# Weight sums by accumulating DMAs, and a reordered end of the MLP, in a two-layer encoder kernel

## The chip, the cores and the metric

One core of a Trainium2 chip runs the whole program in one launch. The metric is the device time of one execution in microseconds, the median of several. The engines are PE (TensorE matmul, with its weight loads shown as PEld), DVE (VectorE), ACT (ScalarE), POOL (GpSimd) and SP (SyncE, which here only issues DMAs).

## The reference

The kernel computes two layers of an encoder on 512 tokens of width 1024, in float32. Per layer:

```
u = RMSNorm(h);  project u with w_in; dilated attention A; retention B
h = h + RMSNorm((sigmoid(ga) * (A @ w_att_out) + sigmoid(gb) * (B @ w_ret_out)) @ w_out)
h = h + RMSNorm(relu(RMSNorm(h) @ w_up)^2 @ w_down)            # the MLP, D_FF = 4096
h = h + sigmoid(RMSNorm(h) @ w_ple_gate) * RMSNorm(p[i] @ w_ple_proj)
```

The change is in the third line alone: in how the weights of the down projection are added up, and in the last eighth of that projection.

## The kernel before

Every matmul is done in three float32r passes: weights and activations are split into a high part (an ACT copy, L273) and the rest (a subtraction on DVE or POOL, L297), and the list HL (L291) names the three products that are kept.

Weights come as 128x1024 blocks of 512 KB in the order of PLAN. `load` (L246) brings raw blocks in from SP into the tag "R" with four buffers; `prefetch` (L266) splits them into "wt" tiles, of which there are five; `chunk` (L285) is called where PE needs a weight and asks for splits up to three items ahead. A weight's split therefore waits until PE is done with the item five places before it.

The up projection makes 32 chunks of 128 features. The down projection of the first seven eighths (UNITS = 7) goes by a Strassen-Winograd scheme in place of plain products: for each unit of 512 features, with token halves and feature halves as a 2x2 of blocks, seven products P1 to P7 replace eight. Some of them need sums of weight blocks: P5 takes b11 + b12, P7 takes b12 + b22, and a chain adds b22 to P5's sum for P6, and b21 to that for P4. `total` (L255) makes these four sums on POOL, in the tag "X" with two buffers. P1, P3 and P2 take single blocks. Per unit the order is up, P1, P5, up, P7, P6, up, P3, P4, up, P2. The products are added up over the units in `prod` (tag "V", L856), and after the last unit seven "folds" (FOLD, L807, run at L905 to L907 on DVE) combine them: the results are P2 and P3 for token tiles 0 and 1, and P4 and P5 for tiles 2 and 3, one for each half of the 1024 columns.

The last eighth of the features is multiplied plainly (L930 to L932), in what the text calls the tail: `row_job` runs the left half of the columns for all four token tiles, weight by weight, then the right half tile by tile. `evac_dn` (L919) adds (left) or subtracts (right) the result into `prod`, takes the sum of squares on ACT, multiplies by the gain (POOL for the left half, DVE for the right), and after the right half calls `pre_norm` (L389) with the residual row h, reloaded from DRAM at L908 to L910 into the tag "A". `pre_norm` makes the normalised row `un`, and queues `rest` (L404): eight transposes of `un` on PE into the two "tp" banks, and the split into `uT` (L412 on ACT, L413 on DVE). `step` (L321), called after each six matmuls, runs the first queued `rest` once it is `age` steps old (AGE_DN = 6 in the tail, eight or seven in the gate stage); `settle` runs what a group of tiles still lacks. The stage behind the tail is the PLE gate ("pg", L953): its first group needs tiles 0 and 1.

PE's order is as written. The order on the other engines and on SP's queue is made by a scheduler that works with its own costs and with priorities: functions under `soon` go ahead by PRIO = 300 places. Each engine's queue is in order on the chip.

Of the kernel before, what the change touches and what calls it, by code (L numbers as in the profile page):

```python
# [12 lines left out]
ALU = mybir.AluOpType  # L13
# [4 lines left out]
P = 128  # L18
S = 512
D = 1024  # L20
NL = 2
NT = S // P
# [19 lines left out]
ALL, PAIRS, ONES = ((0, 1, 2, 3),), ((0, 1), (2, 3)), ((0,), (1,), (2,), (3,))  # L42
# [3 lines left out]
AGE_DN = 6  # L46
# [9 lines left out]
UNITS = 7  # L56


def _dn(e, hf, k):
    return 8 * (e // 2) + 4 * hf + 2 * (e % 2) + k  # L60
# [27 lines left out]
PLAN = [(i,) + x for i in range(NL) for x in PLAN_LAYER]  # L88
# [3 lines left out]
def _items():  # L92
    out = []
    for i in range(NL):
        for kind, c in PLAN_LAYER:
            e = 2 * (c // 8) + c % 4 // 2
            if kind == "up" and c >= 4 and c // 4 <= UNITS:
                e, at = c // 4 - 1, c % 4
                b11, b21, b12, b22 = (CHUNK[i, "dn", _dn(e, hf, k)] for hf in range(2) for k in range(2))
                out.append(((i, "up", c), (CHUNK[i, "up", c],)))  # L100
                out += [((i, p, e), src) for p, src in (
                    (("P1", (b11,)), ("P5", (b11, b12))),
                    (("P7", (b12, b22)), ("P6", ("chain", b22))),
                    (("P3", (b22,)), ("P4", ("chain", b21))),
                    (("P2", (b21,)),),
                )[at]]
            elif kind != "dn" or e >= UNITS:
                out.append(((i, kind, c), (CHUNK[i, kind, c],)))
    return out


ITEMS = _items()
ITEM = {key: m for m, (key, _) in enumerate(ITEMS)}
LAST = {x: m for m, (_, src) in enumerate(ITEMS) for x in src if x != "chain"}


def _qk_cols(base, tile_no, ret):
# [81 lines left out]
def block(ctx: ExitStack, tc: tile.TileContext, x, pT, w, dl, gains, cs, lc, rel, eye, out):  # L199
    nc = tc.nc  # L200
# [11 lines left out]
    def blk(tag, shape, dt=F32, name="blk"):  # L212
        return big.tile(shape, dt, name=name, tag=tag, bufs=NAMES[tag])
# [7 lines left out]
    def bank(tag):  # L221
        b = banks[tag].pop(0)
        banks[tag].append(b)
        return b
# [18 lines left out]
    raw, wt, chain = {}, {}, {}  # L243
    loaded = [0, 0]

    def load(to):  # L246
        while loaded[0] < min(to, len(PLAN)):
            n = loaded[0]
            if len(raw) >= (4 if n < 4 or PLAN[n][1] in ("up", "dn") else 2):
                return  # L250
            raw[n] = blk("A" if n < 4 else "R", [P, D], name="raw")
            nc.sync.dma_start(raw[n], w[n * P:(n + 1) * P, :])
            loaded[0] += 1

    def total(key, src):  # L255
        if src[0] == "chain":
            r, b = chain["sum"], raw[src[1]]
            nc.gpsimd.tensor_tensor(r, r, b, op=ALU.add)  # L258
            return r
        r = blk("X", [P, D], name="wsum")  # L260
        nc.gpsimd.tensor_tensor(r, raw[src[0]], raw[src[1]], op=ALU.add)  # L261
        if key[1] == "P5":
            chain["sum"] = r
        return r

    def prefetch(to_raw, to_split):  # L266
        while loaded[1] < min(to_split, len(ITEMS)):
            m = loaded[1]
            key, src = ITEMS[m]
            load(max([n for n in src if n != "chain"]) + 1)  # L270
            r = raw[src[0]] if len(src) == 1 else total(key, src)
            t = wp.tile([P, 2, 1024], F32R, name="wt", tag="wt", bufs=5)
            nc.scalar.activation(t[:, 0, :], r, AF.Copy)  # L273
            n = src[-1]
            pool = len(src) == 1 and (PLAN[n][1] in POOL_LOW and n % POOL_MOD or PLAN[n][1:] in POOL_MORE)
            for sl in HALVES if pool else (slice(0, D),):
                low(nc.gpsimd if pool else nc.vector, t[:, 1, sl], r[:, sl], t[:, 0, sl])
            wt[m] = t
            loaded[1] += 1
            for n in src:  # L280
                if LAST.get(n) == m:
                    raw.pop(n, None)
        load(to_raw)

    def chunk(*key):  # L285
        m = ITEM[key]
        n = max(x for _, src in ITEMS[max(0, m - 3):m + 4] for x in src if x != "chain")
        prefetch(n + 3, m + 4)
        return wt[m]
# [3 lines left out]
    def low(eng, dst, src, hi, scale=1.0):  # L293
        if scale != 1.0:
            nc.vector.scalar_tensor_tensor(dst, src, scale, hi.bitcast(F32), op0=ALU.mult, op1=ALU.subtract)
        else:
            eng.tensor_tensor(dst, src, hi.bitcast(F32), op=ALU.subtract)  # L297
# [18 lines left out]
    def row_mm(ps, ch, j, lhs, k, t, first, last):  # L316
        for n, (a, b) in enumerate(HL):
            nc.tensor.matmul(ps, lhsT=lhs(a, k, t), rhs=ch[:, b, j * S:(j + 1) * S],  # L318
                             start=first and n == 0, stop=last and n == 2)

    def step(age=None):  # L321
        clock[0] += 1
        age = AGE if age is None else age
        if pending and clock[0] - pending[0][0] >= age:
            soon(pending.pop(0)[1])()
        tick()

    def row_job(keys, lhs, evac, groups=ALL, age=None):
        n = len(keys)
        chs = {}  # L330
        for grp in groups:
            if lhs is u_lhs:
                settle(grp)
            pss = [bank(ROW_BANKS[n]) for n in range(len(grp))]
            for c in range(len(keys)):
                if grp is groups[0]:
                    chs[c] = chunk(*keys[c])
                for t, ps in zip(grp, pss):
                    for j in range(2):
                        row_mm(ps, chs[c], j, lhs, 2 * c + j, t, c == 0 and j == 0, c == n - 1 and j == 1)  # L340
                    if c == n - 1:
                        evac(t, ps)
                    step(age)
# [27 lines left out]
    def soon(f, offset=None):  # L371
        offset = PRIO if offset is None else offset

        def g(*a):
            if not offset:
                return f(*a)
            with tc.high_priority(offset=offset):
                return f(*a)
        return g
# [5 lines left out]
    def settle(ts):  # L385
        while any(t in unready for t in ts):
            soon(pending.pop(0)[1])()
# [247 lines left out]
    def one_layer(i, h):  # L635
# [14 lines left out]
        for c in range(2):  # L650
            b = blk("G", [P, 2, S], name="lct")
# [86 lines left out]
        h = [blk("V", [P, D], name="h") for _ in range(NT)]  # L738
# [3 lines left out]
        for c in range(8):  # L742
            th = ths[c] if c in ths else b_gate(c)
            ps = bank("acc")
            t_job((i, "ro", c), ps, rhs=retT)
            m = t2("m")
            nc.vector.scalar_tensor_tensor(m, th, 1.0, ps, op0=ALU.add, op1=ALU.mult)
            nc.gpsimd.tensor_tensor(fb[c // 2][:, c % 2, :], m, fb[c // 2][:, c % 2, :], op=ALU.add)
        for c in range(8):
            src = fb[c // 2][:, c % 2, :]  # L750
# [31 lines left out]
        for hf in range(2):  # L782
            hsl = slice(hf * S, (hf + 1) * S)
            ch = chunk(i, "pp", hf)
            for t in range(NT):
                ps = bank(PP_BANKS[4 * hf + t])
# [19 lines left out]
        prod = {x: blk("V", [P, 2, S], name=f"sum{x}") for x in PROD}  # L806
# [4 lines left out]
        def dn_bank():  # L811
            b = dn_banks.pop(0)
            dn_banks.append(b)
            return b
# [44 lines left out]
        for j in range(2):  # L859
            settle(PAIRS[j])  # L860
            for c in range(EARLY):
                if not j:
                    early.append(bank(EARLY_BANKS[c]))
                t = chunk(i, "up", c)
# [8 lines left out]
        half_f = []  # L873
# [24 lines left out]
        for e in range(UNITS):  # L898
            ops = operands(*half_f)
            half_f = []  # L900
            for n, xs in enumerate((("P1", "P5"), ("P7", "P6"), ("P3", "P4"), ("P2",))):
                up_job(4 * e + 4 + n)
                for name in xs:
                    product(e, name, ops[name])
                    if e == UNITS - 1:  # L905
                        for to, of in FOLD.get(name, ()):
                            nc.vector.tensor_tensor(prod[to], prod[to], prod[of], op=ALU.add)  # L907
        for t in range(NT):  # L908
            h[t] = blk("A", [P, D], name="hr")
            nc.sync.dma_start(h[t], hm[t])  # L910

        acc = [[prod[x][:, t % 2, :] for x in (("P2", "P3"), ("P4", "P5"))[t // 2]] for t in range(NT)]
# [6 lines left out]
        def evac_dn(hf):  # L919
            @soon  # L920
            def f(t, ps):
                a = acc[t][hf]
                nc.vector.tensor_tensor(a, ps, a, op=ALU.subtract if hf else ALU.add)
                ssq[t][hf] = sumsq(a, t2("junk"), None if hf else 1e-6)
                (nc.vector if hf else nc.gpsimd).tensor_tensor(a, a, g_mpost[:, HALVES[hf]], op=ALU.mult)
                if hf:
                    pre_norm(h[t], t, None, upd_mlp(t, rstd_of(*ssq[t])))
            return f

        for hf in range(2):  # L930
            row_job([(i, "dn", _dn(UNITS, hf, k)) for k in range(2)],
                    lambda a, k, t: half_f[k][:, a, t * P:(t + 1) * P], evac_dn(hf), ONES if hf else ALL, AGE_DN)  # L932

        if not last:
            g_next = gain_row(5 * (i + 1))
# [19 lines left out]
        if last:  # L955
            t, f = NT - 1, evac_pg(1)
            for j in range(CUTS):
                cut = slice(j * S // CUTS, (j + 1) * S // CUTS)
                n = cut.stop - cut.start
                ps = bank("acc")  # L960
# [9 lines left out]
    h = [blk("V", [P, D], name="h") for _ in range(NT)]  # L970
# [25 lines left out]
    for i in range(NL):  # L996
        h = one_layer(i, h)
# [29 lines left out]
```

## Time and profile before

| | |
|---|---|
| time before, median of 3 (lowest to highest) | 1811.55 us (1811.48 to 1811.81) |
| the profiled execution | 1810.16 us |
| its span, first to last instruction | 1808.4 us |
| mean granted TensorE clock | 0.994 |
| busy: PE, DVE, ACT, POOL | 1773.1, 1215.8, 822.1, 496.1 us |
| PE in 40 slices, in tenths | 8999999999999999998999999999999999999989 |
| DMA, mean over the span | 134 GB/s |

Times are from one profiled execution and count from the span's start. A busy PE is not PE at its peak, since matmuls overlap: the interval from one to the next says how fast it goes. The granted clock is 1.00 at 2.4 GHz and 0.50 at 1.2 GHz, and a value between them is a stretch with some of both.

### The profile page before, as it was taken

How to read it: one execution, taken by the hardware profiler on the slowest of the kernel's cores; microseconds unless marked ns; L12 is line 12 of the kernel's file. 1: busy time of each engine (PE TensorE's matmuls, PEld its weight loads, DVE VectorE, ACT ScalarE, POOL GpSimd, SP SyncE). 2: the span in 40 equal slices, each digit the busy share in tenths (PEclk: the TensorE clock that was granted, in tenths of full speed). 3: DMA queues.
4: the chain of work that ended last, by engine and by line, in shares of the span. 5: the costliest groups of instructions: out<-in, count | busy, mean ns of one | idle time of the engine just before them, and what ended most of it. 6: DMA issues, size and time to landing. Idle time of an engine off the chain costs nothing.

```text
span 1808.4 us, 22117 instructions
## 1 busy us (share of the span) xinstructions
PE 1773.1 (98%) x8185; PEld 1466.0 (81%) x8185; DVE 1215.8 (67%) x1839; ACT 822.1 (45%) x1291; POOL 496.1 (27%) x370
## 2 busy tenths in 40 slices
PE   8999999999999999998999999999999999999989
PEld 6888788888888888887888887888888888888867
DVE  6676768743557787788556767677444677777873
ACT  4355454422456454544343555443234574544442
POOL 2312144301165222222023222442012642222130
PEclk9999999999999999999999999999999999999989
DMA  5554464432343222334246545554232422333231
GB/s 214 200 182 157 156 209 148 144 140 93 111 146 117 94 94 97 113 122 158 94 140 212 166 149 171 180 164 169 98 112 97 137 94 99 111 107 104 94 140 47
DMA packets 79165, 243.10 MB, mean 134 GB/s; under 512 B 10961, under 2 KB 19537, under 8 KB 79058
## 3 DMA queue, kind: packets, MB, share of 16 engines
q1 hardware_dynamic: 79058, 241.70, 39.9%
q8 instruction: 64, 1.05, 0.2%
q14 instruction: 43, 0.35, 0.1%
HBM read 208.10 MB, written 33.55 MB: 134 GB/s over the span
## 4 chain that ended last, share of the span: by engine, by line
PE 87%; DVE 5%; POOL 3%; ACT 2%; issue 1%; DMA 1%; SPq 0%; ACTq 0%; POOLq 0%
PE acc L308 27%; PE s L308 17%; PE acc L318 17%; PE acc L845 10%; PE tp L845 5%; PE tp L608 2%; POOL wt L297 2%; PE tp L540 2%; PE tp L503 2%; PE acc L867 1%; ACT wt L273 1%; PE tp L409 1%; PE s L521 1%; DVE wt L297 1%; PE s L522 1%
## 5 line engine op out<-in xcount | busy, mean ns | idle before, releaser
L308 PE MATMUL acc<-uT,wt 128*128 128x512 f32 x1920 | 472.9, 393 | 0.0
L308 PEld LDWEIGHTS acc<-uT,wt 128*128 128x128 f32 x1920 | 356.5, 188 | 71.5
L273 ACT ACTIVATE wt<-raw 128x1024 fp32r<-128x1024 f32 x278 | 293.4, 1056 | 225.6 <-PE acc L308 114.5
L297 DVE TENSOR_TENSOR wt<-raw,wt 128x1024 fp32r<-128x1024 f32 x211 | 291.6, 1389 | 131.5 <-ACT wt L273 130.6
L318 PE MATMUL acc<-wt,uT 128*128 128x512 f32 x1320 | 324.2, 399 | 4.0 <-DVE uT L413 1.7
L308 PE MATMUL s<-uT,wt 128*128 128x512 f32 x1392 | 324.7, 389 | 0.0
L308 PEld LDWEIGHTS s<-uT,wt 128*128 128x128 f32 x1392 | 261.3, 188 | 54.0
L297 POOL TENSOR_TENSOR wt<-raw,wt 128x512 fp32r<-128x512 f32 x134 | 184.9, 1401 | 409.8 <-ACT wt L273 370.6
L318 PEld LDWEIGHTS acc<-wt,uT 128*128 128x128 f32 x1320 | 248.1, 191 | 55.8 <-DVE uT L413 2.9
L845 PE MATMUL acc<-wt,op 128*128 128x512 f32 x792 | 188.0, 389 | 0.0
L845 PEld LDWEIGHTS acc<-wt,op 128*128 128x128 f32 x792 | 148.7, 188 | 30.8
L261 POOL TENSOR_TENSOR wsum<-raw 128x1024 f32<-128x1024 f32 x28 | 74.7, 2667 | 210.1 <-DMA raw<-in_w_dram 210.1
L258 POOL TENSOR_TENSOR wsum<-wsum,raw 128x1024 f32<-128x1024 f32 x28 | 71.1, 2539 | 167.6 <-DVE wt L297 167.6
L856 DVE TENSOR_TENSOR sumP<-acc,sumP 128x512 f32<-128x512 f32 x112 | 75.5, 686 | 61.6 <-PE acc L845 61.1
L884 ACT ACTIVATE relu<-s 128x512 f32<-128x512 f32 x60 | 35.5, 592 | 175.7 <-PE s L308 175.7
L297 DVE TENSOR_TENSOR wt<-wsum,wt 128x1024 fp32r<-128x1024 f32 x56 | 83.9, 1498 | 15.4 <-ACT wt L273 15.4
L845 PE MATMUL tp<-wt,op 128*128 128x512 f32 x384 | 92.3, 389 | 0.0
L308 PE MATMUL acc<-retT,wt 128*128 128x512 f32 x384 | 89.3, 389 | 0.0
L845 PEld LDWEIGHTS tp<-wt,op 128*128 128x128 f32 x384 | 72.1, 188 | 14.9
L308 PEld LDWEIGHTS acc<-retT,wt 128*128 128x128 f32 x384 | 72.1, 188 | 14.9
L300 ACT ACTIVATE rt<-rz 128x512 fp32r<-128x512 f32 x64 | 40.3, 632 | 90.0 <-DVE rz L590 89.5
L526 ACT ACTIVATE z<-z,nm 128x512 f32<-128x512 f32 x64 | 46.2, 722 | 56.6 <-DVE nm L525 56.3
(166 smaller groups left out, 2232.3 us busy)
## 6 DMA issues: line engine op xcount, KB each, us to landing
raw<-in_w_dram SPq DMA_DIRECT2D x292, 512.0 KB, 3.3
kk<-stk SPq DMA_DIRECT2D x128, 128.0 KB, 4.1
stq<-rr SPq DMA_DIRECT2D x16, 512.0 KB, 3.4
qs<-stq SPq DMA_DIRECT2D x128, 64.0 KB, 2.8
stk<-rr SPq DMA_DIRECT2D x16, 512.0 KB, 3.0
stv<-vr SPq DMA_DIRECT2D x16, 512.0 KB, 4.8
vh<-stv SPq DMA_DIRECT2D x16, 512.0 KB, 4.3
gain<-in_gains_dram SPq DMA_DIRECT2D x9, 512.0 KB, 3.8
```

Of the source, the lines that this page charges most:

```text
L258: nc.gpsimd.tensor_tensor(r, r, b, op=ALU.add)
L261: nc.gpsimd.tensor_tensor(r, raw[src[0]], raw[src[1]], op=ALU.add)
L273: nc.scalar.activation(t[:, 0, :], r, AF.Copy)
L297: eng.tensor_tensor(dst, src, hi.bitcast(F32), op=ALU.subtract)
L300: nc.scalar.activation(dst[:, 0], src, AF.Copy, scale=scale)
L308: nc.tensor.matmul(ps, lhsT=t[:, a, (off + k) * P:(off + k + 1) * P], rhs=r, start=k == 0 and n == 0, stop=k == kts - 1 and n == 2)
L318: nc.tensor.matmul(ps, lhsT=lhs(a, k, t), rhs=ch[:, b, j * S:(j + 1) * S], start=first and n == 0, stop=last and n == 2)
L503: nc.tensor.matmul(o, lhsT=v, rhs=pt[k][:, hl, :], start=k == 0 and hl == 0, stop=k == 3 and hl == 1)
L526: nc.scalar.activation(z, z, AF.Exp, bias=nm, scale=-1.0, accum_out=den)
L540: nc.tensor.transpose(ps[:, t * P:(t + 1) * P], zs[t][:, k * P:(k + 1) * P], ident)
L845: nc.tensor.matmul(ps, lhsT=op[:, a, k, j * P:(j + 1) * P], rhs=t[:, b, k * S:(k + 1) * S], start=k == 0 and n == 0, stop=k == 1 and n == 2)
L856: nc.vector.tensor_tensor(a, ps, a, op=ALU.add)
```

## The change

The sums of weight blocks: the first block of P5's and P7's sum is loaded from DRAM into the "X" buffer by SP, and the other block is added onto it by a DMA that POOL issues with `accum_op`; the chain sums are such DMAs alone. Blocks that only sums need are not loaded raw any more, and a raw block is given up after its one split. The folds go from DVE to POOL. The reloaded rows of token tiles 0 and 1 go to "X" in place of "A". The tail takes the token tiles one after the other, each with both halves of the columns, and banks from the rotation of six (four "acc" and two "tp") that the products use.

```diff
-LAST = {x: m for m, (_, src) in enumerate(ITEMS) for x in src if x != "chain"}
+LAST = {src[0]: m for m, (_, src) in enumerate(ITEMS) if len(src) == 1}
...
         while loaded[0] < min(to, len(PLAN)):
             n = loaded[0]
-            if len(raw) >= (4 if n < 4 or PLAN[n][1] in ("up", "dn") else 2):
-                return
-            raw[n] = blk("A" if n < 4 else "R", [P, D], name="raw")
-            nc.sync.dma_start(raw[n], w[n * P:(n + 1) * P, :])
+            if n in LAST:
+                if len(raw) >= (4 if n < 4 or PLAN[n][1] in ("up", "dn") else 2):
+                    return
+                raw[n] = blk("A" if n < 4 else "R", [P, D], name="raw")
+                nc.sync.dma_start(raw[n], rows(n))
             loaded[0] += 1
+
+    def rows(n):
+        return w[n * P:(n + 1) * P, :]
 
     def total(key, src):
         if src[0] == "chain":
-            r, b = chain["sum"], raw[src[1]]
-            nc.gpsimd.tensor_tensor(r, r, b, op=ALU.add)
-            return r
-        r = blk("X", [P, D], name="wsum")
-        nc.gpsimd.tensor_tensor(r, raw[src[0]], raw[src[1]], op=ALU.add)
-        if key[1] == "P5":
-            chain["sum"] = r
+            r = chain["sum"]
+        else:
+            r = blk("X", [P, D], name="wsum")
+            nc.sync.dma_start(r, rows(src[0]))
+            if key[1] == "P5":
+                chain["sum"] = r
+        nc.gpsimd.dma_start(r, rows(src[1]), accum_op=ALU.add)
         return r
...
-            load(max([n for n in src if n != "chain"]) + 1)
+            load(src[-1] + 1)
...
-            for n in src:
-                if LAST.get(n) == m:
-                    raw.pop(n, None)
+            if len(src) == 1:
+                raw.pop(n)
...
-                            nc.vector.tensor_tensor(prod[to], prod[to], prod[of], op=ALU.add)
+                            nc.gpsimd.tensor_tensor(prod[to], prod[to], prod[of], op=ALU.add)
         for t in range(NT):
-            h[t] = blk("A", [P, D], name="hr")
+            h[t] = blk("X" if t < 2 else "A", [P, D], name="hr")
             nc.sync.dma_start(h[t], hm[t])
...
-        for hf in range(2):
-            row_job([(i, "dn", _dn(UNITS, hf, k)) for k in range(2)],
-                    lambda a, k, t: half_f[k][:, a, t * P:(t + 1) * P], evac_dn(hf), ONES if hf else ALL, AGE_DN)
+        tail = [chunk(i, "dn", _dn(UNITS, hf, k)) for hf in range(2) for k in range(2)]
+        for t in range(NT):
+            for hf in range(2):
+                ps = dn_bank()
+                for k in range(4):
+                    row_mm(ps, tail[2 * hf + k // 2], k % 2, lambda a, k, t: half_f[k][:, a, t * P:(t + 1) * P], k, t, k == 0, k == 3)
+                    if k == 3:
+                        evac_dn(hf)(t, ps)
+                    if k % 2:
+                        step(AGE_DN)
```

## Rows read from the trace of the kernel before

**Rows 1.** The page's first part: busy us (share of the span) xinstructions.
```profile
PE 1773.1 (98%) x8185; PEld 1466.0 (81%) x8185; DVE 1215.8 (67%) x1839; ACT 822.1 (45%) x1291; POOL 496.1 (27%) x370
```

**Rows 2.** Waits of PE: who waited for whom: us in total, times, longest.
```profile
PE tp L409 <- DVE ss L349: 12.5, 2, 6.2
```

**Rows 3.** Timeline of PE, layer 0's tail: start, us, engine, line, tiles, xcount [idle before].
```profile
828.93 20.56 PE L318 MATMUL acc<-wt,ff 128*128 128x512 f32 x90
849.69 1.09 PE L409 MATMUL tp<-ident,un 128*128 128x128 f32 x8 [0.20 <-DVE un L399]
...
858.43 1.11 PE L409 MATMUL tp<-ident,un 128*128 128x128 f32 x4 [6.25 <-DVE ss L349]
...
861.76 8.92 PE L318 MATMUL acc<-wt,uT 128*128 128x512 f32 x30
870.52 1.03 PE L409 MATMUL tp<-ident,un 128*128 128x128 f32 x8
871.31 3.00 PE L318 MATMUL acc<-wt,uT 128*128 128x512 f32 x12
```

**Rows 4.** Timeline of PE, layer 1's tail: the first matmuls, and the gate's first.
```profile
1724.06 20.56 PE L318 MATMUL acc<-wt,ff 128*128 128x512 f32 x90
...
1756.89 8.51 PE L318 MATMUL acc<-wt,uT 128*128 128x512 f32 x30
```

**Rows 5.** Timeline of DVE in layer 0's tail.
```profile
829.51 0.68 DVE L856 TENSOR_TENSOR sumP<-acc,sumP 128x512 f32<-128x512 f32 x1
...
841.10 2.09 DVE L297 TENSOR_TENSOR wt<-raw,wt 128x1024 fp32r<-128x1024 f32 x1 [0.34 <-ACT wt L273]
...
843.18 0.67 DVE L923 TENSOR_TENSOR sumP<-acc,sumP 128x512 f32<-128x512 f32 x1
...
847.38 0.68 DVE L923 TENSOR_TENSOR sumP<-acc,sumP 128x512 f32<-128x512 f32 x1
...
854.97 0.88 DVE L399 TENSOR_SCALAR un<-hr,rstd 128x512 f32<-128x512 f32 x2 [0.71 <-POOL rstd L357]
...
857.69 0.68 DVE L413 TENSOR_TENSOR uT<-tp,uT 128x512 fp32r<-128x512 f32 x1
```

**Rows 6.** Windows: us, busy (x) of PE PEld DVE ACT POOL, PEclk, DMA, GB/s.
```profile
862.00:864.00 2.00, 2.00 (x6) 1.57 (x6) 2.00 (x5) 1.71 (x4) 0.00 (x0) 0.50 0.58 164
864.00:866.00 2.00, 2.00 (x7) 1.56 (x6) 1.29 (x3) 0.22 (x2) 1.57 (x2) 0.58 0.24 98
...
1756.90:1760.00 3.10, 3.10 (x9) 2.45 (x8) 3.10 (x6) 1.93 (x5) 0.58 (x1) 0.50 0.00 0
```

**Rows 7.** Windows of layer 0: most of the MLP units, and the tail.
```profile
560.00:828.93 268.93, 268.93 (x1188) 222.69 (x1187) 207.87 (x236) 132.84 (x181) 65.18 (x27) 1.00 0.34 112
...
828.93:861.76 32.83, 24.93 (x113) 20.06 (x112) 25.41 (x43) 15.88 (x36) 12.46 (x18) 0.90 0.42 160
```

**Rows 8.** Groups by line: xcount | busy us, mean ns | idle before, releaser.
```profile
L907 DVE TENSOR_TENSOR sumP<-sumP,sumP 128x1024 f32<-128x1024 f32 x14 | 17.1, 1219 | 0.1
...
L258 POOL TENSOR_TENSOR wsum<-wsum,raw 128x1024 f32<-128x1024 f32 x28 | 71.1, 2539 | 167.6 <-DVE wt L297 167.6
```

**Rows 9.** DMA: landing times of the raw loads, and the queue's packets, MB, share.
```profile
DMA to landing us min/median/max: 3.1/3.3/10.6
...
q1 hardware_dynamic: 79058, 241.70, 39.9%
```

**Rows 10.** Timeline of one MLP unit: chain sums, their splits, and P4's product.
```profile
662.43 2.40 POOL L258 TENSOR_TENSOR wsum<-wsum,raw 128x1024 f32<-128x1024 f32 x1 [1.16 <-DVE wt L297]
...
673.30 1.05 ACT L273 ACTIVATE wt<-wsum 128x1024 fp32r<-128x1024 f32 x1
...
677.35 2.40 POOL L258 TENSOR_TENSOR wsum<-wsum,raw 128x1024 f32<-128x1024 f32 x1 [12.52 <-DVE wt L297]
...
684.22 1.22 DVE L297 TENSOR_TENSOR wt<-wsum,wt 128x1024 fp32r<-128x1024 f32 x1
...
695.65 2.88 PE L845 MATMUL tp<-wt,op 128*128 128x512 f32 x12
```

## Prediction

> **What bounds the kernel now.** I read the busy shares first: TensorE (PE) is busy 98% of the span, VectorE (DVE) 67%, GpSimd (POOL) 27% [rows 1]. So only a stretch in which PE waits, or runs at the lower clock, can give time back, and the waits of PE come next: the largest by far is one wait of 6.25 us in each layer, at the transposes of L409 [rows 2]. The timeline shows where it is [rows 3]. The last eighth of the down projection (the tail) starts at 828.93, and the first PLE-gate matmul of the stage behind it at 861.76, so the tail holds 32.83 us; layer 1 has the same 32.83 (1724.06 to 1756.89) [rows 4]. In those 32.83 us PE does 96 matmuls and 16 transposes. Ninety matmuls last 20.56 us of which the last one's own 0.39 is overlap, so one goes out each 0.2267 us, and 96 are 21.76 us.
>
> Why it waits: token tile 1's normalised row `un` is complete at 854.97 + 0.88 = 855.85, but its transposes start at 858.43, right behind DVE's L413 at 857.69, which reads the last of tile 0 out of the bank "tp" that tile 1 needs [rows 3, 5] (the releaser named, L349, is a tiny DVE instruction right behind it). So two things are late: the chain of a tile (subtract, sum of squares, residual, norm), because the second half of columns goes through the tiles last, and DVE's queue.
>
> The clock is the second loss. PE idles for 6.25 us up to 858.43 [rows 3], and the granted clock is 0.50 (1.2 GHz) in 862 to 864 and 0.58 in 864 to 866; in layer 1 it is 0.50 in 1756.9 to 1760.0 [rows 6]. The matmuls from 861.76 on lose 2.24 × 0.50 + 2 × 0.42 = 1.96 us, in layer 1 3.1 × 0.50 = 1.55 us.
>
> The MLP ahead of the tail is different: PE is busy for all of 268.93 us at clock 1.00 [rows 7]. No change of sums there can gain.
>
> **The change, part by part.**
>
> *Sums by DMA.* In each of 14 units (7 per layer) four POOL additions of 2.5 us on average [rows 8] become four accumulating DMAs issued from POOL, and two of the sums get their first addend by a load of their own from SP; the raw load of b12 goes. Loads per unit go from 8 × 512 KB to 9 + 4 accumulating. The DMA engines' share in the MLP is 0.34 [rows 7]; counting an accumulate twice (it reads the old value too), 17/8 of that is 0.72, so there is room. The open cost is how long an accumulate takes from issue to landing, L. The trace has none. Nearest row: the plain 512 KB load lands in 3.1 us at least, 3.3 in the median, 10.6 at most [rows 9]. Low end 3.1; high end twice the longest, 21.2. I take 5: 3.3 plus a second stream, since 721 us of engine time (39.9% of 1808.4) for 241.7 MB [rows 9] is 1.6 us for 512 KB. Below nothing is excluded: PE has no gap there.
>
> The Trainium skill, "DMA: Bandwidth & Descriptors" (Anatomy of one DMA — SWDGE (gpsimd) path), gives 2.0 us plus bytes over 436 GB/s for a DMA issued from GpSimd, and "Collectives: The Full Stack" (The bandwidth ceiling) halves the rate where the add reads two sources; by these an estimate of L is 2.0 + 2 × 1.2 = 4.4 us, which changes nothing in the sum. No row here shows either.
>
> What L may be, from one unit [rows 10]: the P6 sum starts at 662.43 (when P5's split has read the chain) and ACT reads it at 673.30, so L up to 10.9 costs nothing there. The P4 sum starts at 677.35, PE wants P4 at 695.65, and a split needs about 2.5 us (1.05 on ACT, 1.22 on DVE), so L up to 15.8 fits if P6 is on time. Beyond 10.9 P6's split slips, P4's sum starts later by as much, and with the 4 us from ACT's read at 673.30 to the next sum at 677.35 the limit is where 662.43 + L + 4 + L + 2.5 = 695.65: L = 13.4. Under it the cost is zero, hidden by splits that run five weight buffers ahead; over it each unit stalls by 2 us per us. Waiting on POOL: behind an accumulate that waits for a split or a load stand only other sums, the PLE norms of units 0 and 1 (read in the gate stage) and the last folds. On SP one or two more issues a unit stand between raw loads.
>
> *Folds on POOL.* Seven DVE additions of 1.22 us per layer become POOL additions of about 2.4 [rows 8]. Six are done before their readers, which come more than 5 us into the tail. The last, P1 into P2, can start only after P2's eviction (829.51 + 0.68, so 1.3 us into the tail) [rows 5] and ends at 3.7; tile 0's first half is out of PE at 2.9. DVE waits there for 0.8 us in place of working the fold itself for 1.22: even.
>
> *Tile by tile.* The 96 matmuls stay. Now tile t is complete 5.44 (t+1) us into the tail. Its transposes are due six steps after it was queued (a step is six matmuls, 1.36 us): for tile 0 behind step 9, at 12.24, for tile 1 behind step 13, at 17.68 plus the 0.79 that eight transposes take (870.52 to 871.31 [rows 3]), 18.47. The chains before took 849.69 - 843.18 = 6.5 us for tile 0 and 855.85 - 847.38 = 8.5 us for tile 1, from DVE's subtraction on [rows 3, 5]; with 0.2 us to reach DVE, tile 0 is ready at 12.1 and tile 1 at 19.6. So tile 1 is late by 1.1 us; if DVE's L413 of tile 0 is again last, 858.43 - 855.85 = 2.6 more, 3.7 in all. Below: no wait. I take 2.0 per layer, near the middle, since the rows stand as near to the one end as to the other.
> Without a wait the gate stage starts 21.76 + 2 × 0.79 = 23.34 us after the tail's start, so 32.83 - 23.34 = 9.49 goes per layer, less 2.0 is 7.49. PE no longer idles for six microseconds in one piece, so the clock should stay up: 1.96 and 1.55 more.
> What is late next: all four tail weights live until the last tile, so of five buffers only one holds the next weight ahead; the second gate weight gets its buffer at about 18.5 and is wanted at 23.34 + 2.0 + 2.72 = 28; a split of 2.5 us fits, if DVE is not behind. Tiles 2 and 3 are transposed eight steps after, within the gate stage, with 9 us or more. The residual rows of tiles 0 and 1 now sit in the two "X" buffers, free as soon as the last sum is split, so they come earlier; the next layer's cos/sin tiles lose these buffers until tile 0 and 1 leave the gate stage, but their first reader is 96 + 48 matmuls, 33 us, into that layer: nothing.
>
> *Sum.* 2 × 7.49 + 1.96 + 1.55 = 18.5 us. The profiled execution took 1810.16 (span 1808.4 and 1.76 around it), the median is 1811.55, 1.4 above; I take the difference from the median: 1793.0.
>
> **Rivals.**
> 1. *POOL holds DVE up, and tile 1 misses its place in full.* For: DVE's split took 2.09 us at 841.10 beside POOL's multiplications, against 1.22 elsewhere [rows 5, 10]; the folds put 7 × 2.4 = 17 us of POOL reads next to DVE's work just ahead of the tail. Against: the fold work also leaves DVE. With tile 1 late by 3.7 us and one 2.4 us fold in front of a tail operand, 6.1 in place of 2.0 per layer, with the clock kept: 1793.0 + 8.2 = 1801.
> The Trainium skill, "SBUF — State Buffer" (Who interferes with whom), says that a DVE instruction with two SBUF inputs and a GpSimd instruction that reads SBUF lock each other out for a whole instruction. The 2.09 us agree; by the rule this rival is the one that comes true.
> 2. *DVE is the bound of the tail.* DVE is busy 25.41 of 32.83 us there [rows 7]. Less the 1.22 of a fold, 24.2 us at the same 77% are 31.3: only 1.5 us per layer come back, and the clock still falls: 1808.5, no change. Against: part of that work (tiles 2 and 3) may follow the start of the gate stage.
> 3. *The accumulate is slow (slower than before).* Place: P4's and P6's splits in the 14 units. It decides from L = 13.4 us; each us over costs 14 × 2 = 28 us. At L = 15: 45 us, 1793.0 + 45 = 1838. It turns the whole change slower from about 14.1. For: no accumulate is in the trace, the longest plain load took 10.6, and 13 DMAs share a unit in place of 8. Against: three plain loads of the median fit under 13.4.
> 4. *The sums' part does not do what it says*: PE, without a gap in the MLP, was never late because of POOL's sums, so this part alone is worth nothing; that is in my sum already.
>
> **How the numbers follow.** Forecast 58% (1789.1 with no wait, 1796.5 with 3.7 us of wait per layer and the clock kept). Rival 1 20%, rival 2 6%, rival 3 13%, the rest 3% (a stage elsewhere moved by new orders of ACT, DVE and SP queues), split over faster and slower. The floor is 1811.55 - 2 × 9.49 - 3.51 = 1789.1. The range that leaves out 2 in 10 runs from 1788.5 to 1806: below it almost nothing, above it rivals 2 and 3. A measurement of this kernel tells about 0.2% (3.6 us) from no change. Faster: 58 + 20 + 1 = 0.79; within: 0.06; slower: 0.15.
>
> **What would show it.** In the changed profile: MLP stretches with PE busy throughout, at clock 1.00; accumulates landing in some 5 us; gate stage starting 25 us after the tail's start, granted clock 1.00 there; waits of PE at L409 of 2 us or less. Wrong if PE waits for a split of `wsum` in the MLP (rival 3), if the first gate matmul still comes 30 us after the tail's start (rival 2), or if the clock falls though the gap is small.

## The result, and the profile after

The changed kernel takes 1824.17 us (median of 4 runs, 1823.68 to 1825.29), the kernel before 1811.68 beside it: a ratio of 1.0070, 95% interval 1.0052 to 1.0087. The forecast was 1793.0 us, in a range up to 1806: the change is slower where I had it faster. Line numbers of the changed kernel are higher by 3 to 10: splits L300, products L311 and L848, tail and gate L321, transposes L412, relu squares and ff L891 and L892, folds L910, tail evictions L926.

The page's first part again, for [rows 1]: DVE and POOL are both less busy than before, and the kernel is slower.
```profile
PE 1776.0 (98%) x8185; PEld 1465.5 (80%) x8185; DVE 1185.8 (65%) x1825; ACT 821.6 (45%) x1291; POOL 438.2 (24%) x384
```
Waits of PE in the changed kernel (total, times, longest), for [rows 2]:
```profile
PE acc L321 <- DVE ff L892: 14.0, 2, 7.0
PE acc L321 <- DVE sumP L926: 6.9, 4, 2.6
...
PE tp L412 <- DVE ss L352: 2.6, 2, 1.3
...
PE tp L412 <- DVE un L402: 1.6, 2, 0.8
```
The wait of 6.25 us at the transposes is gone, as the change wanted; what is left at the transposes of the tail is 1.3 and less. In its place PE waits 7.0 us in each layer for `ff`, the last block of relu squares, and 2.6 for a tail eviction. The timeline of PE shows where, for [rows 3, 4]:
```profile
829.13 2.65 PE L321 MATMUL acc<-wt,ff 128*128 128x512 f32 x11
838.73 4.87 PE L321 MATMUL acc<-wt,ff 128*128 128x512 f32 x13 [6.94 <-DVE ff L892]
...
851.19 0.66 PE L412 MATMUL tp<-ident,un 128*128 128x128 f32 x4 [0.79 <-DVE un L402]
852.24 0.66 PE L412 MATMUL tp<-ident,un 128*128 128x128 f32 x4 [0.40 <-DVE sumP L926]
...
860.11 0.66 PE L412 MATMUL tp<-ident,un 128*128 128x128 f32 x4 [1.29 <-DVE ss L352]
...
865.73 1.63 PE L321 MATMUL acc<-wt,uT 128*128 128x512 f32 x6 [0.86 <-DVE sumP L926]
869.93 4.37 PE L321 MATMUL acc<-wt,uT 128*128 128x512 f32 x12 [2.58 <-DVE sumP L926]
...
1730.39 2.65 PE L321 MATMUL acc<-wt,ff 128*128 128x512 f32 x11
...
1766.93 1.62 PE L321 MATMUL acc<-wt,uT 128*128 128x512 f32 x6 [0.85 <-DVE sumP L926]
```
The tail now starts at 829.13 and the gate at 865.73: 36.60 us in place of 32.83 (layer 1: 1766.93 - 1730.39 = 36.54). Windows (length, busy and count of PE, PEld, DVE, ACT, POOL, granted clock, DMA share, GB/s), for [rows 6, 7]:
```profile
560.00:829.13 269.13, 269.13 (x1190) 222.82 (x1188) 186.60 (x226) 132.11 (x179) 39.44 (x30) 1.00 0.60 163
829.13:865.73 36.60, 26.32 (x113) 20.52 (x112) 26.50 (x37) 12.99 (x31) 13.91 (x17) 0.91 0.24 86
...
838.73:843.43 4.70, 4.70 (x13) 3.75 (x14) 0.85 (x2) 0.72 (x2) 1.28 (x1) 0.63 0.37 133
...
870.00:874.00 4.00, 4.00 (x12) 3.22 (x13) 3.56 (x5) 1.79 (x6) 1.23 (x2) 0.63 0.82 253
```
The MLP has no gap, as before. Behind each of the two longest waits of PE, 6.94 and 2.58 us, the granted clock is 0.63: part of the stretch ran at 1.2 GHz.

The span grew by 13.0 us (1808.4 to 1821.4). By the starts of tail and gate in both traces: MLP of layer 0 0.20, tails 3.77 and 3.71, from layer 0's gate to layer 1's tail 2.36 (864.66 against 862.30), from layer 1's gate to the end 2.96 (54.47 against 51.51). All of it lies at the tails and right behind them.

Why `ff` is late stands in the timelines of DVE and POOL just ahead of the tail. DVE:
```profile
811.66 4.54 DVE L300 TENSOR_TENSOR wt<-raw,wt 128x1024 fp32r<-128x1024 f32 x2
817.09 0.69 DVE L859 TENSOR_TENSOR sumP<-acc,sumP 128x512 f32<-128x512 f32 x1 [0.88 <-PE acc L848]
817.70 1.87 DVE L300 TENSOR_TENSOR wt<-raw,wt 128x1024 fp32r<-128x1024 f32 x1
...
820.09 2.29 DVE L891 TENSOR_TENSOR relu<-relu 128x512 f32<-128x512 f32 x1
822.30 0.68 DVE L859 TENSOR_TENSOR sumP<-tp,sumP 128x512 f32<-128x512 f32 x1
822.90 2.28 DVE L892 TENSOR_TENSOR ff<-relu,ff 128x512 fp32r<-128x512 f32 x1
...
825.70 6.16 DVE L300 TENSOR_TENSOR wt<-raw,wt 128x1024 fp32r<-128x1024 f32 x2
...
834.71 3.36 DVE L300 TENSOR_TENSOR wt<-raw,wt 128x1024 fp32r<-128x1024 f32 x1
837.99 0.68 DVE L892 TENSOR_TENSOR ff<-relu,ff 128x512 fp32r<-128x512 f32 x1
```
POOL in the same stretch:
```profile
811.83 18.95 POOL L910 TENSOR_TENSOR sumP<-sumP,sumP 128x1024 f32<-128x1024 f32 x6 [9.84 <-DVE sumP L859]
834.27 2.72 POOL L910 TENSOR_TENSOR sumP<-sumP,sumP 128x1024 f32<-128x1024 f32 x1 [3.49 <-DVE sumP L859]
```
While POOL works its folds, a split on DVE lasts 1.87 to 3.36 us in place of 1.22, and an operation of 512 columns with two SBUF inputs 2.28 in place of 0.68. L859 and L926, whose one input lies in PSUM, stay at 0.68 throughout. POOL's folds last 18.95 / 6 = 3.16 each, where its additions of this shape took 2.40 before [rows 10].

The Trainium skill, "SBUF — State Buffer" (Who interferes with whom), says that a DVE instruction with two SBUF inputs contends with a GpSimd instruction that reads SBUF, that this is an exclusive lock, and that a DVE instruction with at most one SBUF input, outside the two-port performance modes, does not contend. Both halves of the rule show in these rows.

One DVE operation of the tail with a single SBUF tensor is stretched as well: L402, which makes `un` (the input `hr` and one scalar per row).
```profile
849.57 1.28 POOL L928 TENSOR_TENSOR sumP<-sumP,gain 128x512 f32<-128x512 f32 x1
849.63 1.90 DVE L402 TENSOR_SCALAR un<-hr,rstd 128x512 f32<-128x512 f32 x2 [1.03 <-POOL rstd L360]
```
Its two halves take 1.90 us for tile 0 and 1.97 for tile 1, each beside POOL's multiplication by the gain, and 0.87 for tile 2, where that multiplication starts 0.62 us after L402 does. In the kernel before they take 0.88 for every tile ([rows 5] has tile 1's), since the old order has those multiplications done by 844.4, ahead of the first `un`. So the new order of tiles brought a second meeting of DVE and POOL, which no run here takes away; in which mode L402 runs, the trace does not say.

### The profile page after: what moved, and what is told of

The parts are those of the page before. It is cut to its first block, busy times and chain, and to the rows that moved or that the text cites. A ratio compares the mean times of both kernels' runs of the same rounds, so it can differ in the third digit from the quotient of the medians.

```text
span 1821.4 us, 22188 instructions
## 1 busy us (share of the span) xinstructions
PE 1776.0 (98%) x8185; PEld 1465.5 (80%) x8185; DVE 1185.8 (65%) x1825; ACT 821.6 (45%) x1291; POOL 438.2 (24%) x384
## 3 DMA queue, kind: packets, MB, share of 16 engines
q8 instruction: 64, 1.05, 0.2%
## 4 chain that ended last, share of the span: by engine, by line
PE 86%; DVE 6%; POOL 3%; ACT 2%; issue 1%; DMA 1%; SPq 0%; ACTq 0%; POOLq 0%
PE acc L311 27%; PE s L311 17%; PE acc L321 16%; PE acc L848 10%; PE tp L848 5%; PE tp L611 2%; POOL wt L300 2%; PE tp L543 2%; PE tp L506 1%; PE acc L870 1%; DVE wt L300 1%; PE s L524 1%; PE s L525 1%; ACT wt L277 1%; PE tp L412 1%
## 5 line engine op out<-in xcount | busy, mean ns | idle before, releaser
L311 PE MATMUL acc<-uT,wt 128*128 128x512 f32 x1920 | 472.8, 392 | 0.0
L311 PEld LDWEIGHTS acc<-uT,wt 128*128 128x128 f32 x1920 | 356.2, 188 | 71.7
L300 DVE TENSOR_TENSOR wt<-raw,wt 128x1024 fp32r<-128x1024 f32 x211 | 291.9, 1390 | 144.3 <-ACT wt L277 143.4
L321 PE MATMUL acc<-wt,uT 128*128 128x512 f32 x1320 | 324.3, 398 | 10.8 <-DVE sumP L926 6.9
L311 PE MATMUL s<-uT,wt 128*128 128x512 f32 x1392 | 324.7, 389 | 0.0
L311 PEld LDWEIGHTS s<-uT,wt 128*128 128x128 f32 x1392 | 261.1, 188 | 54.1
L321 PEld LDWEIGHTS acc<-wt,uT 128*128 128x128 f32 x1320 | 247.3, 191 | 63.9 <-issue 6.0
L300 POOL TENSOR_TENSOR wt<-raw,wt 128x512 fp32r<-128x512 f32 x134 | 184.4, 1398 | 409.1 <-ACT wt L277 369.8
L848 PE MATMUL acc<-wt,op 128*128 128x512 f32 x792 | 188.0, 389 | 0.0
L848 PEld LDWEIGHTS acc<-wt,op 128*128 128x128 f32 x792 | 148.6, 188 | 30.9
L267 POOL DMA_DIRECT2D wsum<-in_w_dram x56 | 49.4, 884 | 493.5 <-DVE sumP L859 154.1
L859 DVE TENSOR_TENSOR sumP<-acc,sumP 128x512 f32<-128x512 f32 x112 | 75.6, 686 | 64.5 <-PE acc L848 64.0
L300 DVE TENSOR_TENSOR wt<-wsum,wt 128x1024 fp32r<-128x1024 f32 x56 | 70.4, 1256 | 43.4 <-ACT wt L277 43.4
L848 PE MATMUL tp<-wt,op 128*128 128x512 f32 x384 | 92.2, 389 | 0.0
L311 PE MATMUL acc<-retT,wt 128*128 128x512 f32 x384 | 89.3, 389 | 0.0
L311 PEld LDWEIGHTS acc<-retT,wt 128*128 128x128 f32 x384 | 72.1, 188 | 15.0
L848 PEld LDWEIGHTS tp<-wt,op 128*128 128x128 f32 x384 | 72.1, 188 | 15.0
L277 ACT ACTIVATE wt<-wsum 128x1024 fp32r<-128x1024 f32 x56 | 59.2, 1057 | 50.4 <-DMA wsum<-in_w_dram 27.0
```

The lines of the kernel that those rows point to most:

```text
L267: nc.gpsimd.dma_start(r, rows(src[1]), accum_op=ALU.add)
L311: nc.tensor.matmul(ps, lhsT=t[:, a, (off + k) * P:(off + k + 1) * P], rhs=r, start=k == 0 and n == 0, stop=k == kts - 1 and n == 2)
L848: nc.tensor.matmul(ps, lhsT=op[:, a, k, j * P:(j + 1) * P], rhs=t[:, b, k * S:(k + 1) * S], start=k == 0 and n == 0, stop=k == 1 and n == 2)
L859: nc.vector.tensor_tensor(a, ps, a, op=ALU.add)
```

## Experiments

**The change taken apart.** Four kernels, run beside each other and the kernel before (1811.58).

*The whole change, folds back on DVE.*
```diff
-    nc.gpsimd.tensor_tensor(prod[to], prod[to], prod[of], op=ALU.add)
+    nc.vector.tensor_tensor(prod[to], prod[to], prod[of], op=ALU.add)
```


> The changed kernel with its seven folds per layer back on DVE; sums by DMA, tail tile by tile and hr in X stay. Theory L (POOL's folds and DVE's two-input work block each other in the SBUF, so DVE reaches the low half of the last relu block, ff, 7 us late, and the new tail wants that half 2 us after its start): the wait of PE on ff falls from 6.94 to at most 1.5 us per layer, DVE's splits ahead of the tail go back to 1.22 us, and the time to about 1802 (1798 to 1808). Theory T (the tile-by-tile tail is too dense for DVE wherever the folds run): the waits inside the tail stay above 8 us per layer, time 1818 or more.

1808.48 us, ratio 0.9984 (0.9975 to 0.9993). DVE in the same stretch:
```profile
820.56 0.68 DVE L891 TENSOR_TENSOR relu<-relu 128x512 f32<-128x512 f32 x1
...
821.76 0.68 DVE L892 TENSOR_TENSOR ff<-relu,ff 128x512 fp32r<-128x512 f32 x1
...
826.36 2.35 DVE L300 TENSOR_TENSOR wt<-raw,wt 128x1024 fp32r<-128x1024 f32 x2
...
831.57 1.21 DVE L910 TENSOR_TENSOR sumP<-sumP,sumP 128x1024 f32<-128x1024 f32 x1
832.70 0.68 DVE L892 TENSOR_TENSOR ff<-relu,ff 128x512 fp32r<-128x512 f32 x1
```
and PE:
```profile
829.59 2.65 PE L321 MATMUL acc<-wt,ff 128*128 128x512 f32 x11
833.43 3.28 PE L321 MATMUL acc<-wt,ff 128*128 128x512 f32 x13 [1.19 <-DVE ff L892]
...
857.86 1.62 PE L321 MATMUL acc<-wt,uT 128*128 128x512 f32 x6 [0.90 <-DVE sumP L926]
862.06 4.58 PE L321 MATMUL acc<-wt,uT 128*128 128x512 f32 x12 [2.58 <-DVE sumP L926]
```
The one edit gives 15.7 us back. `ff` is ready 832.70 + 0.68 - 829.59 = 3.8 us into the tail, in the changed kernel 837.99 + 0.68 - 829.13 = 9.5. The 5.7 us between add up from DVE's rows: beside POOL its operations grew by 2.19 + 0.65 + 1.61 + 1.60 + 3.81 + 2.14 = 12.0 us, the seven folds that left are 8.5, which leaves 3.5; 0.9 is DVE's wait at 817.09, and one more split (1.2) stands ahead of `ff`: 5.6. The folds cost DVE more from POOL's side than on its own. The expectation's 1802 was too low: what it left out is the wait for L926 at the gate, which the run with turned banks below takes away.

*The kernel before with the new tail alone.*
```diff
-        for hf in range(2):
-            row_job(...)
+        tail = [chunk(i, "dn", _dn(UNITS, hf, k)) for hf in range(2) for k in range(2)]
+        for t in range(NT): ...
```


> The kernel before with the new tail alone (sums on POOL, folds on DVE, hr in A). Theory L: within 2 us of e1_fold_dve, about 1802. Theory T: 1816 or more. Theory S (the sums by DMA cost time by the queues of SP and POOL): some us below e1_fold_dve.

1809.71 us, ratio 0.9990 (0.9981 to 0.9999): 1.9 less, within what a measurement tells from no change. PE waits 1.00 for `ff`, and 0.84 and 2.59 at the gate for L923, the eviction. It lies within 2 us of the version with sums by DMA and folds on DVE, as theory L had it; the 1802 was too low here too. The move of the residual rows to "X" had no run of its own: the two versions, one with it and the sums by DMA and one without, differ by 1.2 us.

*The kernel before with its folds on POOL alone.*
```diff
-    nc.vector.tensor_tensor(prod[to], prod[to], prod[of], op=ALU.add)
+    nc.gpsimd.tensor_tensor(prod[to], prod[to], prod[of], op=ALU.add)
```


> The kernel before with the folds on POOL alone (sums on POOL, old tail). The old tail wants the last ff half 5.4 us after its start. Theory L: DVE is as late as in the changed kernel (ff at 9.5 us), PE waits some 4 us there, part of which the later wait of 7.7 us takes in: 1813 to 1820. Rival (only the new tail is hurt by a late ff): 1812 or less.

1816.37 us, ratio 1.0032 (1.0019 to 1.0044). PE, with the line numbers of before:
```profile
827.95 7.33 PE L318 MATMUL acc<-wt,ff 128*128 128x512 f32 x29
837.01 14.14 PE L318 MATMUL acc<-wt,ff 128*128 128x512 f32 x61 [1.72 <-DVE ff L889]
...
859.65 1.11 PE L409 MATMUL tp<-ident,un 128*128 128x128 f32 x4 [6.24 <-DVE ss L349]
```
`ff` comes 9.06 us into the tail here, nearly as late as in the whole change (9.6), but the old order of the tail wants it 7.33 us in (the expectation had 5.4), the new one 2.65. So the same lateness costs 1.72 here and 6.94 there. This is the interaction: the parts alone cost -0.4 (sums), -1.9 (tail) and +4.8 (folds), in sum +2.5, and together +12.5.

*The kernel before with the sums by DMA alone*, their loads as in the change.
```diff
+        nc.gpsimd.dma_start(r, rows(src[1]), accum_op=ALU.add)
```


> The kernel before with the sums by accumulating DMAs alone (folds on DVE, old tail, hr in A). Theories L and T: no difference, 1811.7 within 1.5, PE without a gap in the MLP. Theory S: above 1814.

1811.20 us, ratio 0.9998 (0.9989 to 1.0007): no difference, as [rows 7] had it: PE had no gap there to close.

**The wait for the eviction at the gate.** The gate's first two tiles take the two accumulator banks that tile 3, the last of the tail, was just written to. To the version with folds on DVE, one turn of the bank list by two ahead of the gate:
```diff
+        for _ in range(2):
+            bank("acc")
         if not last:
```


> e1_fold_dve with the list of the four acc banks turned by two ahead of the gate stage, so that the gate's first two tiles take the banks of token tile 2 and not those of tile 3, the last of the tail. Theory B (what is left in e1 is mostly the wait of 0.9 + 2.58 us for DVE's L926 of tile 3, which empties the bank that the gate wants, and the low clock behind it): both waits fall under 1 us, the clock stays at 1.00 in the gate's first matmuls, 2 x (3.0 + 1.7) = 9 us less than e1: 1799 (1797 to 1802). Theory T (DVE is behind anyway, so the next wait takes the place): 1804 or more.

1800.80 us, ratio 0.9943 (0.9931 to 0.9956): faster than both kernels, and within the expected 1797 to 1802. PE, and the windows of its tail and of the first 10 us of its gate:
```profile
856.42 3.11 PE L321 MATMUL acc<-wt,uT 128*128 128x512 f32 x13
861.00 1.43 PE L321 MATMUL acc<-wt,uT 128*128 128x512 f32 x5 [1.48 <-DVE wt L300]
```
```profile
829.26:856.42 27.16, 24.54 (x114) 19.49 (x112) 19.63 (x33) 11.99 (x29) 9.08 (x13) 1.00 0.29 108
856.42:866.42 10.00, 8.52 (x42) 6.81 (x41) 9.55 (x16) 6.56 (x15) 3.24 (x5) 1.00 0.38 132
```
No wait for L926 is left at the gate; the longest wait of PE there is 1.48 us (1.73 in layer 1), and the granted clock is 1.00. That wait is for the low part of the second gate weight, whose split on DVE starts at 858.71 and lasts 2.25 us beside POOL's L928 (858.53, 1.33 us) in place of 1.22.

*The same turn in the kernel before with the new tail alone*, sums on POOL as they were (same edit):

> The kernel before with the new tail and the turned list of accumulator banks alone: sums and folds as before (POOL's additions for the sums, DVE's for the folds). If the sums are off the path, as 1811.2 against 1811.6 said for them alone, this is as fast as the version with the sums by DMA (1800.8): 1801 (1799 to 1803), tail of 27.2 us. If the accumulating DMAs free POOL or DVE for the new tail after all, it stays several us slower, 1804 to 1808, with a longer wait of PE for the last ff block.

1800.42 us, ratio 0.9949 (0.9936 to 0.9961). The first reading held: the gain is the tail's and the banks'; the sums by DMA have no part in it. The profiled execution, at 1805.65 the slowest of the five, has a tail of 28.0 us in place of the expected 27.2: tile 1 waits 1.28 there, with its L399 beside POOL.

*The same turn in the changed kernel*, folds on POOL (same edit):

> The changed kernel whole, folds on POOL, with only the list of accumulator banks turned by two ahead of the gate. If the ff wait and the bank wait are two separate losses that add, the 0.4 and 0.9 and 2.6 us behind L926 go in both layers and the ff wait of 7 us stays: 1824 less 7 or 8, 1816.5 (1814 to 1819). If the bank wait is only what the late ff leaves over (DVE late in everything), most of it moves to another wait and the time stays above 1820.

1817.11 us, ratio 1.0035 (1.0022 to 1.0047). Against the kernel before beside each (1811.27 here, 1810.82 for the version with turned banks), the turn takes the changed kernel from +12.5 to +5.8 us and the version with folds on DVE from -3.1 to -10.0: 6.7 and 6.9 go, and PE still waits 7.18 us for `ff`: two separate losses. The folds' place costs 5.8 + 10.0 = 15.8 us here.

**Order or lock.** A rival to the lock is that DVE has `ff` behind splits that aren't urgent. Changed kernel, the two DVE operations of the last relu blocks moved ahead:
```diff
-    nc.vector.tensor_tensor(r, r, r, op=ALU.mult)
-    nc.vector.tensor_tensor(b[:, 1, :], r, b[:, 0, :].bitcast(F32), op=ALU.subtract)
+    soon(nc.vector.tensor_tensor)(r, r, r, op=ALU.mult)
+    soon(nc.vector.tensor_tensor)(b[:, 1, :], r, b[:, 0, :].bitcast(F32), op=ALU.subtract)
```


> The changed kernel (folds on POOL) with the two DVE operations for the low half of the last relu blocks put ahead in priority, nothing else. Theory L (locks make DVE late as a whole; the order of its queue adds to that): DVE still comes out of the two locked splits 3 us into the tail, so PE waits 2.5 to 4 us on ff in place of 6.94, and the clock stays up there: 1824.2 - 2 x 5 = 1814 (1811 to 1818). Rival O (the order alone, the pg split ahead of ff, makes the wait): ff wait under 1 us, time near e1_fold_dve, 1808.5.

1823.59 us, ratio 1.0072 (1.0059 to 1.0084): no gain; the expected 1814 was wrong. PE waits 5.63 us for `ff` and 1.28 for a split that it pushed back. `ff` now stands ahead of the last split, and DVE is late all the same: the splits ahead of the tail still last 4.56, 2.83 and 5.53 us. But the run is no clean test of the order, since the edit has a cost of its own: the split of the last sum waits 4.17 us for ACT, where it waited 0.62 in the changed kernel, and this lateness shows again below without any fold on POOL. An estimate without it, from how much later DVE reaches the first split ahead of the tail (13.9 us before the tail's start, in place of 17.5), leaves a wait of some 3.6 us, as theory L had it and not under 1 as rival O.

*Folds as accumulating DMAs* from SBUF to SBUF, issued from POOL, which then reads no SBUF (the P2 fold on DVE):
```diff
-    nc.gpsimd.tensor_tensor(prod[to], prod[to], prod[of], op=ALU.add)
+    (nc.vector.tensor_tensor(prod[to], prod[to], prod[of], op=ALU.add) if name == "P2"
+     else nc.gpsimd.dma_start(prod[to], prod[of], accum_op=ALU.add))
```


> The changed kernel with six of the seven folds as accumulating DMAs inside the SBUF, issued from POOL, and the last (P1 into P2) on DVE: neither POOL nor DVE reads the six. Theory L: with no POOL instruction reading the SBUF, DVE's splits ahead of the tail take 1.22 us, the wait on ff falls to 1.5 us or less, time as e1_fold_dve within 3: 1806 to 1811. Rival O or a plain lack of DVE time: no better than 1816. If such a DMA takes much longer than the 5.4 us of the sums, the wait shows at L926 of tile 0's right half instead.

1823.87 us, ratio 1.0068 (1.0053 to 1.0082). Its folds (KB each, us from issue to landing), and two rows each of DVE and PE:
```profile
sumP<-sumP POOLq DMA_DIRECT2D x12, 512.0 KB, 6.8
```
```profile
823.38 2.34 DVE L300 TENSOR_TENSOR wt<-raw,wt 128x1024 fp32r<-128x1024 f32 x2
...
845.15 0.69 DVE L926 TENSOR_TENSOR sumP<-acc,sumP 128x512 f32<-128x512 f32 x1 [8.20 <-DMA sumP<-sumP]
```
```profile
834.33 3.24 PE L321 MATMUL acc<-wt,ff 128*128 128x512 f32 x13 [1.00 <-DVE ff L892]
...
852.67 2.17 PE L412 MATMUL tp<-ident,un 128*128 128x128 f32 x8 [8.30 <-DVE un L402]
```
With POOL off SBUF the two splits are back at 2.34 and the wait for `ff` at 1.00: the lock is shown by taking it away. The scheduler also put the last split behind `ff` here; of the 3.36 us that it lasted ahead of `ff` in the changed kernel, 1.22 belong to that order and 2.14 to the lock. The time did not follow, since the folds hang on one another, 6.8 us each in the median, and the last to land holds the eviction of tile 0's right half by 8.2 us, as the expectation's last sentence had it.

**What is left of the tail.** To the version with turned banks, the moved `ff` operations and transposes due eight steps after a tile in place of six:
```diff
-                        step(AGE_DN)
+                        step(AGE_DN + 2)
```


> f1_banks, with the two DVE operations for the low half of the last relu blocks put ahead in priority, and the transposes of the tail due 8 steps after in place of 6. Theory B: the waits of 1.2 (ff) and of 0.78 + 0.40 + 0.26 to 1.3 (tiles 0 and 1) go as well, 2 x 2.5 us below f1_banks: 1794 (1791 to 1797). Theory T: within 2 us of f1_banks.

1817.35 us, ratio 1.0034 (1.0023 to 1.0046): 16.6 us slower than without, a miss. The two edits were then run apart. *The age alone:*

> The version with turned banks, and only the age at which a tail tile's transposes are due raised from six steps to eight; the DVE order is left. If the later transposes were what cost 16.5 us in the run that had both edits, this takes about 1815, with PE waiting for DVE uT and ACT uT at the transposes of tiles 2 and 3 in the gate stage. If the earlier ff operations were what hurt, this takes 1799 to 1802. I lean to the second by three to two: a later age only moves work that has slack.

1810.89 us, ratio 0.9996 (0.9987 to 1.0005). My lean fell. PE, and a window:
```profile
856.09 1.54 PE L321 MATMUL acc<-wt,uT 128*128 128x512 f32 x6
859.78 0.74 PE L321 MATMUL acc<-wt,uT 128*128 128x512 f32 x2 [2.15 <-ACT uT L415]
863.53 4.63 PE L321 MATMUL acc<-wt,uT 128*128 128x512 f32 x10 [3.01 <-DVE uT L416]
```
```profile
863.00:868.00 5.00, 4.47 (x11) 3.41 (x12) 4.56 (x7) 1.09 (x3) 1.77 (x2) 0.50 0.21 66
```
The gate starts 26.11 us into the tail, 1.05 sooner, and then waits 2.15 and 3.01 for the transposed tiles, and falls to the lower clock. Waits taken out of the tail came back larger behind it.

*The moved `ff` operations alone:*

> The version with turned banks, and only the two DVE operations that make the low part of each of the last ff blocks moved ahead in DVE's order. The complement of the run with the age alone: if the moved ff operations push the weight splits behind them and so starve PE, about 1812 with an ff wait near 3.3 us; if the age was at fault, 1798 to 1801 with an ff wait under 0.5 us.

1809.31 us, ratio 0.9990 (0.9982 to 0.9999), with an `ff` wait of 3.36: moving `ff` ahead made it later. One row each of ACT and DVE in this kernel:
```profile
810.20 1.06 ACT L277 ACTIVATE wt<-wsum 128x1024 fp32r<-128x1024 f32 x1 [4.50 <-DMA wsum<-in_w_dram]
811.29 1.23 DVE L300 TENSOR_TENSOR wt<-wsum,wt 128x1024 fp32r<-128x1024 f32 x1 [4.14 <-ACT wt L277]
```
The split that stands here ahead of the next relu block waits 4.14 us for ACT's half; in the version with turned banks the same split starts at 807.82 after 0.80. All behind it on DVE shifts by those three microseconds. ACT's half comes later because it waits 4.50 us for the accumulating DMA of the last sum. The moved operations push back the split that this DMA waits for, so POOL issues it at 802.41 in place of 801.24, and it lands 7.8 us after its issue in place of 5.5; that the two raw loads issued at 802.94 beside it made it slower is likely, but not shown. So the sums by DMA are harmless only as long as nothing urgent stands behind their splits in DVE's queue. Against the kernel before beside each, the two edits cost 9.6 (age) and 8.1 (`ff`) apart and 16.6 together.

## Why the prediction was wrong

**The failed step is "Folds on POOL ... even".** It counted a fold as 2.4 us on POOL against 1.22 off DVE, and of seven only the last, against tile 0's eviction. Its claim that six are done before their readers held (the sixth ends at 830.78). What it did not count is what POOL's reads do to DVE's other work in those 19 us: splits and relu blocks grew by 12.0 us, more than the 8.5 that left DVE. Rival 1 named this mechanism, but priced it as one 2.4 us fold ahead of a tail operand, with the clock kept; here seven folds act on a queue whose last product, `ff`, is the tail's own operand. That cost 6.94 us of wait per layer, where the version with folds on DVE waits 1.19; by the times, the folds' place costs 15.7 us of the 31.2 that the forecast is off.

**The tile order moved a demand that the text did not follow.** It followed what becomes ready sooner (tile 0's chain) and not what is wanted sooner: the last `ff` block 2.65 us into the tail in place of 7.33. Alone that costs about 1 us, with late folds 7.

**The gate's banks.** "What is late next" looked at weights and transposes, not at the accumulator banks: 0.86 and 2.58 us per layer behind tile 3's eviction, about 7 us in all by the two runs with turned banks. Its clause "if DVE is not behind" failed too: with the banks turned, PE waits 1.48 us for the second gate weight.

**The sum against the trace.** Per tail I had 25.34 us (23.34 and 2.0 of waits). Measured 36.60: waits 6.94 + 0.79 + 0.40 + 1.29 + 0.86 = 10.28, so 8.28 more than 2.0; PE busy 26.32, so 2.98 more than 23.34, of which 26.32 - 24.54 = 1.8 is against the version with turned banks, mostly the 13 matmuls behind the wait (4.87 us against 3.24 with `ff` nearly in time); the other 1.2 is in that version too. That is 11.26 and, for layer 1, 11.20. Behind the gate's start I had a gain of 1.96 and 1.55 from the clock and it lost 2.36 and 2.96: 4.32 and 4.51, with the 2.58 us of the bank wait in each. In sum 31.3, and 1824.2 - 1793.0 is 31.2.

**The other rivals.** The sign set for rival 2 came (the gate starts over 30 us after the tail), but not its cause: DVE is busy 26.50 of 36.60 us, and with its own folds back and the banks turned the tail takes 27.16. Rival 3 did not come: accumulates land in 5.4 us.

**What held.** The sums: accumulates land in 5.4 us in the median against the 5 taken, at most 9.4 against the limit of 13.4, the DMA share in the MLP is 0.60 against 0.72, and the MLP keeps its 0 us of gaps. The limit counts what PE needs and not what stands behind a sum's split on DVE; in the run with `ff` moved ahead 7.8 us was already too long. For [rows 9], the accumulates' issue on POOL (ns, least/median/most) and landing:
```profile
L267 POOL DMA_DIRECT2D wsum<-in_w_dram x56: 858/874/1072, 350.9 to 1702.4; - x56
...
DMA to landing us min/median/max: 5.1/5.4/9.4
```
The estimate of 4.4 us from the Trainium skill's "DMA: Bandwidth & Descriptors" (Anatomy of one DMA — SWDGE (gpsimd) path) and "Collectives: The Full Stack" (The bandwidth ceiling) was a little low. The tile chains: 0.79 + 0.40 + 1.29 = 2.48 us of waits per layer against 2.0, near by luck: the text had tile 0 in time and tile 1 alone late. Both wait where L402 is stretched by 1.0 us beside POOL; where tile 1's L402 takes 0.88 (with folds on DVE, layer 0), its wait is 0.26. "The clock should stay up" is true of the tail once no long wait is in it (1.00 in the version with turned banks), and false of the change as it is. The forecast of 1793 stays 7.8 us under the best version: its tail takes 27.16 against 25.34, and its gate waits 1.48 us for a split.

Open is how much of the remaining loss is clock and how much is wait: no run here held one and changed the other.

## What to carry to other kernels

Work moved from DVE to POOL is not gone from DVE: price it by every DVE operation with two SBUF inputs that runs in the same stretch (here L402 with one as well), and by the operand that stands last in DVE's queue. When an order of work is changed so that something is ready sooner, list also what is wanted sooner, operands and banks, and when each is ready. Parts that cost little alone (+2.5 us in sum here) can cost 12.5 together, so run them in pairs, not only one by one. A change that brings one operand forward in a queue pushes others back: look at what those release, down to the DMAs.

## What the hardware showed that was not expected

An accumulating DMA of 512 KB from SBUF to SBUF took 6.8 us in the median, from DRAM 5.4, a plain raw load of that size 3.3 before [rows 9] and 3.7 in the changed kernel; the issue of one took 0.87 us on POOL. Two splits in a row beside POOL's folds took 6.16 us, near the 6.32 of two folds of 3.16, and seven operations of DVE with two SBUF inputs stand beside the six folds: in that stretch DVE went at POOL's pace. An operation with one SBUF tensor, L402, took 1.90 us beside POOL's multiplication and 0.88 without.
